# A hybrid mixer block: side work of the last block dealt anew, and the first rows of the output phase loaded ahead of w_out

## The chip, the cores and the metric

The kernel runs on one core of a Trainium2 chip. Its five engines work side by side, each through its own list of instructions in a fixed order: TensorE (PE, matmuls and transposes), VectorE (DVE), ScalarE (ACT), GpSimd (POOL) and the queue of SyncE (SP), which issues nearly all transfers between HBM and the core's memory. They wait for one another by semaphores. The metric is the device time of one execution in microseconds, the median of several runs.

## The reference

One decoder layer on x of 2048 tokens by 1024 channels, all in float32. A row norm with an adaptive scale and shift gives h; one projection `h @ w_in` gives the columns of three token mixers, which all read the same h:

```
A: gMLP.  y_a = gelu(u) * (tril(W_s) @ rms(gelu(v)) + b_s) * silu(z)      4 groups x 64, chunks of 128 tokens
B: mLSTM. q, k = silu(causal_conv(.)); per chunk of 128 tokens and 4 heads x 96:
          h = (intra-chunk weights @ v + w_inter * C q) / max(|den|, exp(-m));  C = decay * C + k^T v
          y_b = sigmoid(o) * rms(h) * silu(z)
C: stick-breaking attention, 6 heads x 64, strictly causal, with normed q and k:
          z = q k^T / 8;  a = sigmoid(z) * (product of sigmoid(-z) over the later keys)
          y_c = (a @ v) * silu(z_gate)
out = x + gate * (concat(y_a, y_b, y_c) @ w_out)
```

## The kernel before

The 2048 tokens are 16 tiles of 128, in three blocks of 5, 5 and 6 tiles (`BLOCKS`); the change touches the last block (tiles 10 to 15) and the phase behind it. Matmul operands are split in a high and a low part (the code has them side by side in `hT`, `wr`, `Kst`, `Vst`, `Qst`, `aT`, `wo`), so each product is three matmuls.

In a block, the attention goes through three **pairs** of heads (p = 0, 1, 2; the first, second and third pair below). `c_proj` projects q, k and v of the pair for the block's tiles; then `stick(p, ...)` does the attention in **units**: one tile of queries, one head, up to four tiles of keys, from the latest keys back. A unit is named pair_tile_head_firstkeytile, as in `z0_13_1_8`. With six tiles a pair has 44 units, the three pairs 132. A unit goes through `front` (TensorE: scores `z`; ScalarE: `bb` and `be`, two sigmoids; VectorE: a scan over `bb`, L414; then `be * bb`, L418, on VectorE and POOL by turns), `middle` (TensorE transposes into `at`; ScalarE and VectorE make the two parts of `aT`, L431 and L432), `back` (TensorE: `av`) and `fin` (`py`, `yc`, a store to `y_d`). The buffers `bb`, `be` and `aT` have four copies each.

Beside the attention runs **side work**: projections for the other two mixers, each one **chunk** of 6 tiles x 8 x 3 matmuls of 384 columns: `bqk_proj` (two chunks; PSUM tiles `pb`; its evacuation has four VectorE instructions per tile, L501 and L504, on `acc`), `bg_proj` (two, `pg`), `cz_proj` (`pcz`), `a_proj` (two, `pa`; a chain of VectorE, ScalarE and POOL instructions behind each tile, and two products `psp`/`gu` at its end) and `bv_proj` (`pv`). All these PSUM tiles and those of `c_proj` come from one pool of three buffers (`pproj`). Their weights come through `wr` (11 buffers, 8 used by a chunk). The list `fillers` says which chunks go beside which pair, and `interleave` takes steps from it in proportion to the cost so far; `behind` first finishes the pair's own `c_proj`. In the last block, `gating()` (the mLSTM gates' logarithms and maxima, small VectorE and ScalarE work on `g_all` and `g_row`) is mixed into the first pair and `first_chunk()` into the second.

The order of each engine's list is then fixed by a scheduler that places every instruction when its model finds it ready, by priority, so that later work can come earlier where an engine would be free: `bv_proj`, in the code behind the third pair, is placed within it.

The **output phase** (from `rs.close()` on) reuses the memory of the phase before: the pool `ld` lies where `stg`, `wr` and `hT` were, which side work uses to its end, and `wk`, `wo` and `wkb` where the attention's tiles were. `load(i)` fetches a tile's rows: `qk2`, `vb`, `gt`, `y`, `x` (`qk2` and `vb` only for i > 0); `wst` is `w_out` as loaded, which `split_wo` takes apart into `wo` (ScalarE casts the high part, VectorE and POOL subtract). Then, tile after tile, `mlstm(i)` runs the chunk of mixer B (`wT`, `s`, `pT`, `k`, `kw`, `i`, `nd`, `n`, `c`, `C`), `mixed(i)` makes the rows of y, `turned(i)` transposes them (`pty`, `yT`) and `out_proj(i)` multiplies with `wo` (`po`).

Of the kernel before, what the change touches and what calls it, by code (L numbers as in the profile page):

```python
# [33 lines left out]
def hybrid_block_kernel(ctx: ExitStack, tc: tile.TileContext, x, c, norm_g, w_ada, b_ada, w_in,  # L34
# [300 lines left out]
    def behind(cp, rest):  # L335

        yield from cp
        for m, c in enumerate(rest):
            if m == 6 and pend:
                evac_finish()  # L340
            yield c
        if pend:
            evac_finish()
# [128 lines left out]
    def stick_cost(t0, nb):  # L472
        return sum(2 * ((i + 1) * (2 * P / 2.4 + 218) + 215) for i in range(t0, t0 + nb))
# [34 lines left out]
    def bv_proj(t0, nb):  # L508
        with prio(HIGH[0]):
            wt = weights(w_in[0], [(OFF["bv"], 384)])  # L510
        for j in range(nb):
            i = t0 + j
            ps = pproj.tile([P, 512], F32, tag="proj", name=f"pv{i}")
            yield from proj_tc(ps[:, :384], wt, j, 384)
            vb = t512(f"vb{i}")
            vv = vb[:, 0:388].rearrange("p (h e) -> p h e", h=4)
            nc.gpsimd.memset(vv[:, :, 96:97], 1.0)
            nc.scalar.copy(vv[:, :, 0:96], ps[:, :384].rearrange("p (h e) -> p h e", h=4))
            nc.sync.dma_start(vb_d[i * P:(i + 1) * P, :], vb[:, 0:388])
# [230 lines left out]
    def run(g):  # L750
        for _ in g:
            pass
# [5 lines left out]
    def mix(a, n, g):  # L758
        for m, c in enumerate(a):
            yield c  # L760
            if m % n == n - 1:
                yield next(g, 0)
        yield from g

    def interleave(main, main_cost, side, side_cost):

        done = 0.0
        used = [0.0]
        side = iter(side)

        def step():
            c2 = next(side, None)
            if c2 is None:
                used[0] = 1e30
            else:
                used[0] += c2

        def until(j):
            with prio(-STK):
                while ready[0] < j:  # L780
                    step()

        need[0] = until
        while True:
            with prio(STK):
                c = next(main, None)
            if c is None:
                break
            done += c
            while used[0] < done / main_cost * side_cost:  # L790
                step()
        run(side)
# [46 lines left out]
    for b, nb in enumerate(BLOCKS):  # L839
        last = b == len(BLOCKS) - 1  # L840
        chunk = nb * KT * 3 * 384 / 2.4
        HIGH[0] = 0 if b == 0 else -4000
        fillers = [
            (chain(bqk_proj(t0, nb, 0), bqk_proj(t0, nb, 1), bg_proj(t0, nb, 0)), 3),
            (chain(bg_proj(t0, nb, 1), cz_proj(t0, nb), a_proj(t0, nb, 0)), 3),
            (a_proj(t0, nb, 1), 1),
        ]
        if b == 1:
            fillers[0] = (mix(fillers[0][0], 8, gate_gemv()), 3)
        if last:  # L850
            fillers[0] = (mix(fillers[0][0], 36, gating()), 3)
            fillers[1] = (mix(fillers[1][0], 14, first_chunk()), 3)
        for p in range(3):
            lead = min(nb, 2 + b)
            if p > 0:
                ready[0] = -1
                cp = c_proj(b, t0, nb, p)
                for _ in range(lead * KT + 1):
                    next(cp)
            cp_cost = 0 if b == 0 and p == 0 else (nb - lead) * KT * 3 * 384 / 2.4  # L860
            if b == 0 and p == 0:
                HIGH[0] = -400
            if p == 2 and not last:
                get_x(t0 + nb, 0)
                get_x(t0 + nb + 1, 1)
            interleave(stick(p, t0, nb), stick_cost(t0, nb), behind(cp, fillers[p][0]), cp_cost + fillers[p][1] * chunk)
        tail = bv_proj(t0, nb)
        if last:
            run(tail)
        else:  # L870
            t1, n1 = t0 + nb, BLOCKS[b + 1]
            ready[0] = -1
            cp = c_proj(b + 1, t1, n1, 0)
            lead = min(n1, 3 + b)
            for m, _ in enumerate(chain(tail, islice(cp, lead * KT + 1))):
                j = m // KT - 1
                if 0 <= j < n1 and m % KT in (1, 5):
                    if m % KT == 1 and j + 2 < n1:
                        get_x(t1 + j + 2, j + 2)
                    hT_half(t1 + j, j, m % KT // 4)  # L880
        t0 += nb
# [138 lines left out]
                next(side, None)  # L1020
        run(side)

    for kp in range(KT // 2):
        if kp == 1:
            load(0)
        nc.sync.dma_start(wst[kp], w_out[0, kp * 256:(kp + 1) * 256, :].rearrange("(a p) f -> p a f", p=P))
    load(1)
    C0 = wk.tile([96, 4, 97], F32, tag="C", name="C0")
    nc.sync.dma_start(C0.rearrange("p h e -> p (h e)"), c_d)
    CT = [C0]  # L1030
    wkb = ctx.enter_context(tc.tile_pool(name="wkb", bufs=2, side="right"))
    psO = ctx.enter_context(tc.tile_pool(name="psO", bufs=2, space=PSUM))
# [49 lines left out]
```

## Time and profile before

| | us |
|---|---|
| median of 3 runs (1473.59 to 1475.47) | 1473.66 |
| the profiled execution | 1471.23 |
| its span, first to last instruction | 1469.2 |
| TensorE busy (share) | 1393.4 (95%) |
| VectorE busy | 1018.8 (69%) |
| ScalarE busy | 676.5 (46%) |
| POOL busy | 647.6 (44%) |

In the span the last block's first pair lies at about 730 to 906 us, the second at 906 to 1078, the third at 1078 to 1209, and the output phase from there to the end. Times in rows are microseconds from the start of the span. Matmuls overlap in the array, so a matmul's own duration is longer than its distance to the next; distances between starts tell what it costs. The chain that ended last is 66% TensorE and 15% VectorE.

### The profile page before, as it was taken

What the parts mean: (1) busy time and instruction counts of PE and PEld (TensorE: products, weight loads), DVE (VectorE), ACT (ScalarE), POOL (GpSimd) and SP (SyncE); (2) the same over time, 40 slices, a digit from 0 to 9 for tenths busy, and PEclk for the clock granted to TensorE, in tenths of its full rate; (3) what the DMA queues carried; (4) which work ended last, traced back from release to release, by engine and by line L of the source; (5) the groups of instructions that cost most, each with busy time, mean ns of one, the idle gap of its engine ahead of it and who ended that gap; (6) DMA issues with size and microseconds to landing.
All of it is one profiled execution on the core that took longest, in us unless ns stands there. A gap on an engine that the chain in (4) does not pass through costs nothing.

```text
span 1469.2 us, 24957 instructions
## 1 busy us (share of the span) xinstructions
PE 1393.4 (95%) x8468; PEld 1298.2 (88%) x8468; DVE 1018.8 (69%) x1778; ACT 676.5 (46%) x1656; POOL 647.6 (44%) x1140
## 2 busy tenths in 40 slices
PE   5999999898999999999999999999999978999998
PEld 3789999798999999988999899989999867888887
DVE  6797554676995666588799976778778788444543
ACT  3364454453554444346467655556455655111110
POOL 4473553743433432554343343434445337435442
PEclk8999999999999999999999999999999999999999
DMA  9866776666535533633433344303432435555541
GB/s 324 293 204 206 237 228 197 208 202 236 191 128 176 198 116 124 222 100 127 148 105 126 104 146 137 102 15 120 157 102 69 156 113 153 178 160 154 175 154 58
DMA packets 187103, 233.19 MB, mean 159 GB/s; under 512 B 22714, under 2 KB 160344, under 8 KB 186976
## 3 DMA queue, kind: packets, MB, share of 16 engines
q1 hardware_dynamic: 186752, 231.59, 48.5%
q8 instruction: 67, 1.10, 0.3%
q14 instruction: 60, 0.49, 0.1%
q0 software_dynamic: 224, 0.02, 0.0%
HBM read 159.24 MB, written 72.31 MB: 158 GB/s over the span
## 4 chain that ended last, share of the span: by engine, by line
PE 66%; DVE 15%; DMA 6%; issue 5%; POOL 4%; ACT 2%; SPq 1%; POOLq 0%; DVEq 0%; ACTq 0%
DVE bb L414 5%; PE av L444 5%; PE at L429 4%; PE pc L297 4%; PE pc L299 4%; PE pc L298 4%; PE po L995 4%; PE po L997 3%; PE po L996 3%; PE pg L297 3%; PE pg L298 3%; PE pg L299 3%; DMA st<-in_w_in_dram 2%; PE z L401 2%; PE z L402 2%
## 5 line engine op out<-in xcount | busy, mean ns | idle before, releaser
L414 DVE TENSOR_TENSOR_SCAN bb<-bb,bb 128x513 f32<-128x513 f32 x144 | 191.3, 1328 | 25.5 <-ACT bb L406 24.7
L418 POOL TENSOR_TENSOR be<-be,bb 128x512 f32<-128x512 f32 (+3 forms) x120 | 133.0, 1108 | 132.9 <-DVE bb L414 81.4
L432 DVE TENSOR_TENSOR aT<-at,aT 128x512 fp32r<-128x512 f32 (+3 forms) x240 | 142.3, 598 | 39.8 <-ACT aT L431 39.1
L406 ACT ACTIVATE bb<-z 128x512 f32<-128x512 f32 (+3 forms) x240 | 130.2, 543 | 80.5 <-PE z L402 61.2
L444 PE MATMUL av<-aT,Vst 128*128 128x256 f32 x816 | 148.7, 295 | 17.8 <-DVE aT L432 13.0
L431 ACT CAST aT<-at 128x512 fp32r<-128x512 f32 (+3 forms) x240 | 126.6, 529 | 83.8 <-PE at L429 82.7
L444 PEld LDWEIGHTS av<-aT,Vst 128*128 128x128 f32 x816 | 119.9, 189 | 30.1 <-DVE aT L432 21.0
L429 PE MATMUL at<-ident,be 128*128 128x128 f32 x816 | 132.7, 274 | 5.2 <-DVE aT L432 2.3
L297 PE MATMUL pc<-wr,hT 128*128 128x384 f32 (+1 forms) x384 | 134.8, 355 | 2.8 <-ACT hT L290 1.3
L299 PE MATMUL pc<-wr,hT 128*128 128x384 f32 (+1 forms) x384 | 134.7, 351 | 1.6 <-DVE hT L291 1.5
L298 PE MATMUL pc<-wr,hT 128*128 128x384 f32 (+1 forms) x384 | 133.4, 347 | 0.0
L407 ACT ACTIVATE be<-z 128x512 f32<-128x512 f32 (+3 forms) x240 | 131.7, 549 | 0.0
L429 PEld LDWEIGHTS at<-ident,be 128*128 128x128 f32 x816 | 99.2, 141 | 14.2 <-DVE aT L432 3.7
L995 PE MATMUL po<-wo,yT 128*128 128x512 f32 x256 | 104.9, 410 | 0.3 <-ACT yT L984 0.3
L414 DVE TENSOR_TENSOR_SCAN bb<-bb 128x129 f32<-128x129 f32 (+3 forms) x96 | 87.1, 911 | 23.3 <-POOL bb L409 16.8
L405 POOL MEMSET bb<- 128x1 f32 x240 | 23.5, 100 | 177.6 <-DVE bb L414 123.6
L996 PE MATMUL po<-wo,yT 128*128 128x512 f32 x256 | 101.6, 397 | 0.0
L997 PE MATMUL po<-wo,yT 128*128 128x512 f32 x256 | 101.4, 399 | 0.0
L487 PE MATMUL pb<-hT,wr 128*128 128x320 f32 (+1 forms) x288 | 93.2, 324 | 1.2 <-DMA wr<-w_d 1.2
L489 PE MATMUL pb<-hT,wr 128*128 128x320 f32 (+1 forms) x288 | 92.1, 323 | 1.8 <-DVE wr L191 1.3
L297 PE MATMUL pa<-wr,hT 128*128 128x384 f32 x256 | 88.2, 347 | 5.1 <-DVE qk L360 2.4
L401 PE MATMUL z<-Kst,Qst 128*128 128x512 f32 (+3 forms) x240 | 90.2, 385 | 2.4 <-DVE Kst L371 1.6
(273 smaller groups left out, 3900.3 us busy)
## 6 DMA issues: line engine op xcount, KB each, us to landing
wr<-w_d SPq DMA_DIRECT2D x160, 384.0 KB, 5.6
w_d<-wr SPq DMA_DIRECT2D x80, 384.0 KB, 3.4
wad<-in_w_ada_dram SPq DMA_DIRECT2D x8, 1024.0 KB, 6.7
xo<-in_x_dram SPq DMA_DIRECT2D x16, 512.0 KB, 3.8
out_dram<-o SPq DMA_DIRECT2D x31, 256.0 KB, 2.9
xt<-in_x_dram SPq DMA_DIRECT2D x15, 512.0 KB, 4.9
st<-in_w_in_dram SPq DMA_DIRECT2D x60, 128.0 KB, 3.4
wr<-w_d SPq DMA_DIRECT2D x16, 392.0 KB, 6.2
```

The lines of the kernel that those rows point to most:

```text
L297: nc.tensor.matmul(ps, lhsT=hT[:, 0, k, cols], rhs=wt[k][:, 0, :W], start=k == 0, stop=False)
L298: nc.tensor.matmul(ps, lhsT=hT[:, 0, k, cols], rhs=wt[k][:, 1, :W], start=False, stop=False)
L299: nc.tensor.matmul(ps, lhsT=hT[:, 1, k, cols], rhs=wt[k][:, 0, :W], start=False, stop=k == KT - 1)
L407: nc.scalar.activation(be[:, :w], z[:, :w], AF.Sigmoid)
L414: nc.vector.tensor_tensor_scan(rev, rev, rev, carry.get((i, h), 1.0), ALU.mult, ALU.bypass)
L418: eng.tensor_tensor(be[:, :w], be[:, :w], bb[:, 1:w + 1], ALU.mult)
L429: nc.tensor.transpose(at[:, s, :], be[:, s * P:(s + 1) * P], ident)
L432: nc.vector.tensor_tensor(aT[:, :nb_, 1, :], at[:, :nb_, :], aT[:, :nb_, 0, :].bitcast(F32), ALU.subtract)
L444: nc.tensor.matmul(flat(av), lhsT=Vst[:, s0 + s, h, :], rhs=flat(aT[:, s]), start=(s0 + s == i), stop=(s0 + s == 0))
L995: nc.tensor.matmul(po, lhsT=yT[:, 0, k, :], rhs=wo[k][:, 0, cs], start=k == 0, stop=False)
L996: nc.tensor.matmul(po, lhsT=yT[:, 0, k, :], rhs=wo[k][:, 1, cs], start=False, stop=False)
L997: nc.tensor.matmul(po, lhsT=yT[:, 1, k, :], rhs=wo[k][:, 0, cs], start=False, stop=k == KT - 1)
```

## The change

Two edits. In the last block the side work is dealt anew: the first pair gets the two `bqk_proj` chunks (before: these and `bg_proj`'s first half), the second `bg_proj`'s two halves and `cz_proj` (before: `bg_proj`'s second half, `cz_proj` and `a_proj`'s first half), the third both `a_proj` and `bv_proj` (before: `a_proj`'s second half, with `bv_proj` in the code behind the pair). For the third pair `interleave` is told 0.8 of the attention's cost, so that the side work is to be used up at four fifths of it. The steps at which `gating()` is mixed in go from every 36th to every 24th. In the output phase the rows of tiles 0 and 1 are loaded first, and then `w_out`, in column halves: the four left halves and then the four right ones.

```diff
@@ -845,10 +845,16 @@
             (chain(bg_proj(t0, nb, 1), cz_proj(t0, nb), a_proj(t0, nb, 0)), 3),
             (a_proj(t0, nb, 1), 1),
         ]
+        if last:
+            fillers = [
+                (chain(bqk_proj(t0, nb, 0), bqk_proj(t0, nb, 1)), 2),
+                (chain(bg_proj(t0, nb, 0), bg_proj(t0, nb, 1), cz_proj(t0, nb)), 3),
+                (chain(a_proj(t0, nb, 0), a_proj(t0, nb, 1), bv_proj(t0, nb)), 3),
+            ]
         if b == 1:
             fillers[0] = (mix(fillers[0][0], 8, gate_gemv()), 3)
         if last:
-            fillers[0] = (mix(fillers[0][0], 36, gating()), 3)
+            fillers[0] = (mix(fillers[0][0], 24, gating()), 2)
             fillers[1] = (mix(fillers[1][0], 14, first_chunk()), 3)
@@ -863,11 +869,9 @@
-            interleave(stick(p, t0, nb), stick_cost(t0, nb), behind(cp, fillers[p][0]), cp_cost + fillers[p][1] * chunk)
-        tail = bv_proj(t0, nb)
-        if last:
-            run(tail)
-        else:
+            interleave(stick(p, t0, nb), stick_cost(t0, nb) * (0.8 if last and p == 2 else 1), behind(cp, fillers[p][0]), cp_cost + fillers[p][1] * chunk)
+        if not last:
+            tail = bv_proj(t0, nb)
@@ -1020,13 +1024,14 @@
-    for kp in range(KT // 2):
-        if kp == 1:
-            load(0)
-        nc.sync.dma_start(wst[kp], w_out[0, kp * 256:(kp + 1) * 256, :].rearrange("(a p) f -> p a f", p=P))
+    load(0)
     load(1)
     C0 = wk.tile([96, 4, 97], F32, tag="C", name="C0")
     nc.sync.dma_start(C0.rearrange("p h e -> p (h e)"), c_d)
+    for n in range(2):
+        for kp in range(KT // 2):
+            cs = slice(n * 512, (n + 1) * 512)
+            nc.sync.dma_start(wst[kp][:, :, cs], w_out[0, kp * 256:(kp + 1) * 256, cs].rearrange("(a p) f -> p a f", p=P))
```

The scheduler turns this into other lists. Three places follow; a row is the line, the operation, the tile it writes, those it reads, and the shape (x4: four in a row).

TensorE in the first pair, at the unit of tile 13, head 1, latest keys; `pb` is side work of `bqk_proj`, `z`, `at` and `av` belong to the attention. Before:

```order
L489 MATMUL pb4_10_1_10049<-hT_130,wr25_6_9744 128x384
L487 MATMUL pb4_10_1_10049<-hT_130,wr25_7_9746 128x384
L488 MATMUL pb4_10_1_10049<-hT_130,wr25_7_9746 128x384
L489 MATMUL pb4_10_1_10049<-hT_130,wr25_7_9746 128x384
L487 MATMUL pb5_10_0_10144<-hT_130,wr25_0_9732 128x384
L401 MATMUL z0_13_1_12_9912<-Kst_443,Qst_126 128x256
L402 MATMUL z0_13_1_12_9912<-Kst_443,Qst_126 128x256
L444 MATMUL av0_12_1_9752<-aT0_12_1_4_9776,Vst_444 128x256 x4
L429 MATMUL at0_13_0_12_9850<-ident_74,be0_13_0_12_9758 128x128 x2
L488 MATMUL pb5_10_0_10144<-hT_130,wr25_0_9732 128x384
L489 MATMUL pb5_10_0_10144<-hT_130,wr25_0_9732 128x384
L487 MATMUL pb5_10_0_10144<-hT_130,wr25_1_9734 128x384
```

And now, at the same unit:

```order
L401 MATMUL z0_13_1_12_9782<-Kst_443,Qst_126 128x256
L402 MATMUL z0_13_1_12_9782<-Kst_443,Qst_126 128x256
L401 MATMUL z0_13_1_8_9828<-Kst_443,Qst_126 128x512
L402 MATMUL z0_13_1_8_9828<-Kst_443,Qst_126 128x512
L444 MATMUL av0_12_1_9637<-aT0_12_1_4_9658,Vst_444 128x256 x4
L429 MATMUL at0_13_0_12_9729<-ident_74,be0_13_0_12_9643 128x128 x2
L401 MATMUL z0_13_1_4_9859<-Kst_443,Qst_126 128x512
L402 MATMUL z0_13_1_4_9859<-Kst_443,Qst_126 128x512
L444 MATMUL av0_12_1_9637<-aT0_12_1_0_9703,Vst_444 128x256 x4
L429 MATMUL at0_13_0_8_9759<-ident_74,be0_13_0_8_9675 128x128 x4
L460 MATMUL py0_12_9773<-fold_79,avt0_12_0_9608 128x64
L444 MATMUL av0_13_0_9770<-aT0_13_0_12_9732,Vst_444 128x256 x2
```

The side matmuls between the units are gone from this stretch: from `z0_13_0_8` to `z0_14_0_0`, 11 units, no projection stands in TensorE's order.

TensorE in the third pair, where the side work ends; `pv15` is the last tile of `bv_proj`. Before:

```order
L298 MATMUL pv15_14742<-wr33_7_14595,hT_130 128x384
L299 MATMUL pv15_14742<-wr33_7_14595,hT_130 128x384
L444 MATMUL av2_13_0_13857<-aT2_13_0_12_13822,Vst_444 128x256 x2
L460 MATMUL py2_12_13860<-fold_79,avt2_12_1_13834 128x64
L401 MATMUL z2_13_1_0_13970<-Kst_443,Qst_126 128x512
L402 MATMUL z2_13_1_0_13970<-Kst_443,Qst_126 128x512
L429 MATMUL at2_13_0_4_13900<-ident_74,be2_13_0_4_13813 128x128 x4
L444 MATMUL av2_13_0_13857<-aT2_13_0_8_13854,Vst_444 128x256 x4
```

And now:

```order
L298 MATMUL pv15_14504<-wr33_7_14150,hT_130 128x384
L299 MATMUL pv15_14504<-wr33_7_14150,hT_130 128x384
L429 MATMUL at2_14_0_0_14403<-ident_74,be2_14_0_0_14302 128x128 x4
L401 MATMUL z2_15_0_12_14508<-Kst_443,Qst_126 128x512
L402 MATMUL z2_15_0_12_14508<-Kst_443,Qst_126 128x512
L444 MATMUL av2_14_0_14325<-aT2_14_0_4_14366,Vst_444 128x256 x4
L429 MATMUL at2_14_1_12_14445<-ident_74,be2_14_1_12_14348 128x128 x3
L401 MATMUL z2_15_0_8_14549<-Kst_443,Qst_126 128x512
```

The end of the side work moved from ahead of the unit `z2_13_1_0`, with 17 of 44 units to come, to ahead of `z2_15_0_12`, with 8 to come.

ScalarE where the output phase begins; `yc2_15` is the attention's last tile, `wT` the weights of mixer B, `yT` the transposed rows of tile 0. Before:

```order
L462 COPY yc2_15_14578<-py2_15_14575 128x128
L663 ACT_TABLE_LOAD
L663 ACTIVATE wT1_14927<-wT1_14927,gT_96 128x128 x4
L663 ACTIVATE wT2_15044<-wT2_15044,gT_96 128x128 x4
L984 CAST yT0_14849<-pty0_0_14850 128x512
L984 CAST yT0_14849<-pty0_1_14857 128x512
L901 CAST wo0_14799<-wst0_14807 128x512
```

And now:

```order
L462 COPY yc2_15_14768<-py2_15_14765 128x128
L663 ACT_TABLE_LOAD
L663 ACTIVATE wT1_14931<-wT1_14931,gT_96 128x128 x3
L988 CAST yT0_14853<-pty0_0_14854 128x512
L988 CAST yT0_14853<-pty0_1_14861 128x512
L905 CAST wo0_14799<-wst0_14807 128x512
L905 CAST wo1_14800<-wst0_14807 128x512
```

`yT` moved ahead of the second tile's exponentials and of one of the first tile's; those follow behind all sixteen casts of `wo`. On TensorE, in the same way, `n1`, `s2`, `k3` and `i3` of mixer B moved from ahead of the first `po` to behind it.

## Rows read from the trace of the kernel before

**Rows 1.** Windows: length; busy us (count) of PE, PEld, DVE, ACT, POOL; clock; DMA; GB/s.

```profile
730.00:906.00 176.00, 172.39 (x1089) 165.52 (x1088) 144.43 (x243) 110.72 (x239) 70.71 (x143) 1.00 0.35 113
906.00:1078.00 172.00, 168.67 (x1070) 161.39 (x1069) 128.07 (x213) 88.49 (x212) 69.32 (x136) 1.00 0.33 106
1078.00:1209.00 131.00, 118.93 (x755) 108.61 (x754) 108.87 (x170) 80.39 (x187) 54.60 (x113) 1.00 0.33 111
1160.00:1209.00 49.00, 37.21 (x240) 29.47 (x239) 44.05 (x57) 31.85 (x67) 18.68 (x35) 1.00 0.51 178
971.00:981.00 10.00, 7.61 (x50) 5.68 (x50) 10.00 (x17) 7.58 (x19) 4.70 (x13) 1.00 0.01 2
1209.00:1219.00 10.00, 7.49 (x64) 6.85 (x63) 5.07 (x11) 5.52 (x14) 4.72 (x6) 0.98 0.93 253
1219.00:1226.00 7.00, 7.00 (x31) 6.32 (x31) 7.00 (x8) 7.00 (x14) 6.41 (x6) 0.54 0.45 138
```

**Rows 2.** Timeline of TensorE in the third pair: start, duration, instruction.

```profile
1150.67 0.39 PE L401 MATMUL z<-Kst,Qst 128*128 128x512 f32 x1
1150.90 0.40 PE L402 MATMUL z<-Kst,Qst 128*128 128x512 f32 x1
...
1160.49 0.34 PE L298 MATMUL pv<-wr,hT 128*128 128x384 f32 x1
1160.67 0.34 PE L299 MATMUL pv<-wr,hT 128*128 128x384 f32 x1
...
1205.82 0.60 PE L429 MATMUL at<-ident,be 128*128 128x128 f32 x4
1206.17 0.72 PE L444 MATMUL av<-aT,Vst 128*128 128x256 f32 x4
```

**Rows 3.** VectorE's groups by form in 740 to 1209: count, busy, mean, idle before.

```profile
L414 DVE TENSOR_TENSOR_SCAN bb<-bb,bb 128x513 f32<-128x513 f32 x94 | 125.1, 1331 | 16.3 <-ACT bb L406 15.7
L432 DVE TENSOR_TENSOR aT<-at,aT 128x512 fp32r<-128x512 f32 x108 | 72.5, 677 | 17.5 <-ACT aT L431 17.4
L418 DVE TENSOR_TENSOR be<-be,bb 128x512 f32<-128x512 f32 x44 | 31.2, 710 | 0.6
L501 DVE SCALAR_TENSOR_TENSOR acc<-xb,prm,acc 128x384 f32<-128x384 f32 x36 | 23.8, 662 | 1.1 <-ACT acc L497 0.9
```

**Rows 4.** Waits in 1160 to 1210: total us, times, longest.

```profile
POOL y L968 <- DMA y<-yb_d: 1.5, 1, 1.5
```

**Rows 5.** Timeline of TensorE: last av group, first output matmul, the second tile's first.

```profile
1207.82 0.74 PE L444 MATMUL av<-aT,Vst 128*128 128x256 f32 x4 [0.28 <-DVE aT L432]
...
1222.02 0.77 PE L995 MATMUL po<-wo,yT 128*128 128x512 f32 x1
...
1246.32 0.47 PE L995 MATMUL po<-wo,yT 128*128 128x512 f32 x1
```

**Rows 6.** Timeline of ScalarE at the seam.

```profile
1213.73 1.28 ACT L663 ACT_TABLE_LOAD   x1 [3.10 <-DMA wT<-m_d]
1215.02 2.45 ACT L663 ACTIVATE wT<-wT,gT 128x128 f32<-128x128 f32 x8
1217.38 1.04 ACT L984 CAST yT<-pty 128x512 fp32r<-128x512 f32 x2
```

**Rows 7.** Timeline of POOL: its last three subtractions for the left halves.

```profile
1221.82 4.21 POOL L902 TENSOR_TENSOR wo<-wst,wo 128x512 fp32r<-128x512 f32 x3
```

**Rows 8.** Timeline of SyncE's queue: first and last load, and C0.

```profile
1161.04 0.38 SPq L1026 DMA_DIRECT2D wst<-in_w_out_dram  x1
...
1180.30 0.32 SPq L921 DMA_DIRECT2D gt<-gate_d  x1
...
1208.79 0.48 SPq L1029 DMA_DIRECT2D C<-c_d  x1
```

**Rows 9.** The page's DMA issues: count, KB each, us to landing.

```profile
wad<-in_w_ada_dram SPq DMA_DIRECT2D x8, 1024.0 KB, 6.7
xo<-in_x_dram SPq DMA_DIRECT2D x16, 512.0 KB, 3.8
```

## The prediction

> **What bounds the kernel now.** I read the page's busy shares first (TensorE 95% busy, so only holes in TensorE are worth anything), then windows over the last block's three attention pairs and the start of the output phase, then the timelines of the engines at its seams. In the first and second pair TensorE stands idle for 3.6 us and 3.3 us, in the third for 12.1 us [rows 1]. Nearly all of that is one stretch: the last side matmul (`pv15`) starts at 1160.67 [rows 2], and from then the attention runs alone. In 1160 to 1209 VectorE is busy for 44.1 of 49 us and TensorE for 37.2 [rows 1]: 11.8 us of holes, with VectorE in charge. A full unit costs VectorE one scan (1.33 us), one `aT` subtraction (0.68) and half of the `be` products (0.71 / 2): 2.37 us [rows 3]. TensorE needs less for it: two 512-column matmuls 0.23 us apart and eight small ones at 0.09 to 0.14 each [rows 2], which I take as 0.12: about 1.44 us. So a unit with nothing beside it costs TensorE 0.9 us of waiting.
>
> But VectorE is nearly full early too. In 730 to 906 it is busy for 144 of 176 us [rows 1], and there `bqk_proj` alone adds 36 taps of 0.66 us, 24 us [rows 3], while `bg_proj` has a single product a tile there.
>
> The second place is the seam to the output phase: the last attention matmul group starts at 1207.82 and the first output matmul at 1222.02 [rows 5]. ScalarE waits there 3.1 us for `wT`, spends 2.45 us on eight exponentials, and only then casts `yT` at 1217.38 [rows 6].
>
> **The change, part by part.** *The deal of the side work.* A chunk is 144 matmuls of 384 columns, 0.17 to 0.18 us apart [rows 2]: 24.4 us of TensorE. `bg_proj`'s first half leaves the first pair, one `a_proj` leaves the second for the third, and `bv_proj` stays in the third. In the order before, 17 units still follow `pv15`; in the changed order 8 do, so the 4/5 is what the order does (36 of 44 units).
>
> What this is worth I worked out pair by pair. I cut the 132 units of the block into groups of four, added for each group TensorE's issue times (384 columns 0.17, 512 columns 0.226, small ones 0.124) and VectorE's mean durations per form over the instructions that the order puts between the two scans, and took the larger. Before, the three pairs have TensorE sums of 167, 162 and 106 us, VectorE sums of 158, 139 and 113, and larger-of-two sums of 178, 170 and 124: 472 together. The trace took 470 between the same scans, so the method holds for before. Changed, TensorE has 147, 149 and 139, VectorE 157, 122 and 131, and the larger-of-two sums are 172, 156 and 147: 475.
>
> So the first pair gives up 20 us of TensorE work but gets only 6 us shorter, since VectorE keeps all its work. The order shows where: from z0_13_0_8 on, 11 units run with no side matmul between them, since `acc`'s evacuation stands late in VectorE's order, after `gating`, and the three PSUM buffers of the projections are then full. Over twelve units there, 801 to 831 us in the trace of before, the sums are now 18.7 us for TensorE and 35.1 for VectorE. The hole has moved from the end of the third pair to the middle of the first. The net is +3.3 us. With groups of 2 to 11 units, and with TensorE's costs 6% lower, the same sum gives -3.3 to +6.6: these are my bounds.
>
> *Rows ahead of w_out.* POOL waited 1.5 us for `y` of tile 0 before its product [rows 4], while `be` products stood behind it on its queue; that `y` was issued after the first 1 MB of `w_out`. In the changed order these rows come first and the product stands one unit after the loads start. I take -1.0 us (bounds -1.5 and 0; the lower is the row, nothing is gained if VectorE has slack there).
>
> *w_out in halves.* Eight transfers of 512 KB take the place of four of 1 MB. The nearest rows are 3.8 us for 512 KB and 6.7 us for 1 MB [rows 9]: one after the other 30.4 against 26.8 us, 3.6 us more. What hides it: before, the loads' first and last issue are 19 us apart (1161.04 and 1180.30 [rows 8]). Now 8 units follow `pv15`, 8 x 2.37 = 19 us, and the drain, from the last scores to the last `av` group, is some 8 us more: 27 us, and a further 10 us pass before the first cast of `wo`. I take 0. If the cover is gone, up to 3.6 us show. The Trainium skill ("DMA: Bandwidth & Descriptors", section Bandwidth) says to batch transfers to 1 MiB or more, as smaller ones pay a larger share of fixed cost, and so speaks against the halves; by it these loads get longer, which is the case of late loads below. The trace agrees in direction (138 GB/s against 157, from the same two rows).
>
> *The start of the output phase.* Three things move in the order. `gu1`'s two products and stores leave the seam; I count that at nothing, since `avt` behind them waits for ScalarE anyway. On ScalarE `yT` comes after 3 exponentials in place of 8: 5 x 0.3 = 1.5 us earlier. On TensorE `n1`, `s2`, `k3` and `i3` no longer stand ahead of the first output matmul, so it waits for `yT` and the first `wo` halves alone: I get 9.5 us after the last `av` group, against 14.2 [rows 5]. From there POOL's `wo` subtractions set the pace, whose first halves end at 1226.03 [rows 7], 18.2 us after that group; they come 1.5 to 2 us earlier. The second tile's output starts at 1246.32 [rows 5], 38.5 us after the last `av` group; what lies in between shows 2.5 us of idle TensorE in 1209 to 1219 and 7 us at a mean granted clock of 0.54 in 1219 to 1226 [rows 1]. Counting the changed order through to `po1` I get 33 to 35 us. I take -3.5 us. Bounds: 0, if `wT1` (whose load still waits for the end of attention and now queues behind more rows) holds `yT` where it was; -8, if all idle time and half-clock time goes.
>
> **The sum.** +3.3 - 1.0 - 3.5 = -1.2 us. The profiled execution took 1471.23 us for a span of 1469.2, so it would take 1470.0; the median of the runs is 1473.66, 2.4 us above the profiled one, and becomes 1472.5. Changes under 0.2% (2.9 us) can't be told from none here.
>
> **Rivals.** *Faster: the first pair's backlog is worked off under the change-over.* After each pair comes `c_proj` of the next, with TensorE full and VectorE less so. If VectorE's late `acc` work slides in there, groups of 8 or 11 units are the right ones (-3.3 to -1.2) and the sum is -3.3 - 1.0 - 3.5 = -7.8: 1466. For it: TensorE is full in 730 to 906 except for 3.6 us though VectorE has 144 us of work. Against: TensorE is in order, and 11 units without side work stand in its order in one run.
>
> *Slower: every stretch pays for itself.* The attention has four `bb` and four `be` buffers, so the engines can't drift apart by more than about three units, 7 us of VectorE work. The empty run holds 35.1 - 18.7 = 16 us of excess, beyond that. Then +6.6 is right, and the seam gives half of its estimate: +6.6 - 1.0 - 1.8 = +3.8: 1477.5; without the seam's gain 1479. It decides if TensorE's idle time in the first pair rises by more than 15 us. Against: groups of four reproduce before within 2 us.
>
> *The clock falls in the empty run.* In 971 to 981, 7.6 of 10 us busy, the granted clock stayed at 1.00; after 1209 to 1219, 7.5 of 10 us busy, it was 0.54, part of the time the lower level of 1.2 GHz [rows 1]. At half clock 18.7 us of TensorE work becomes 37, against 35.1 of VectorE: 2 us at worst. It widens the range only.
>
> *Late w_out (slower).* If the halves land after the first casts of `wo`, the 3.6 us show: 1476.
>
> *No effect as said* is excluded by the order: the side work does end after 36 units.
>
> **How the numbers follow.** Forecast, within 0.2%: 0.40. Faster: 0.34. Slower: 0.23 for stretches that pay for themselves and 0.03 for late loads, 0.26. The single terms' bounds add to 1473.66 - 3.3 - 1.5 - 8 = 1461 and 1473.66 + 6.6 + 0 + 3.6 = 1484; both ends need everything to go one way, so for 8 in 10 I take 1464 to 1480.5. The likeliest case's own range is 1470.7 to 1476.6.
>
> **What would show it.** Right: TensorE's idle time in the first pair rises to 10 to 20 us, in one run of 11 units with VectorE at 95% or more; the third pair's end has 5 to 6 us of holes in place of 11.8; first output matmul 9 to 11 us after the last `av` group; no wait of POOL for `y`. Wrong: the first pair shorter by 12 us or more (faster), or the third longer by over 27 us (slower); `wo` casts waiting for a DMA; first output matmul still 14 us after.

## The result, and the profile after

The changed kernel takes 1487.77 us (median of 4 runs, 1486.61 to 1489.93) beside 1474.27 for the kernel before on the same chip (4 runs): 1.0095 times as long, 95% interval 1.0082 to 1.0108, or 13.5 us more. The forecast was 1472.5 (1464 to 1480.5). The profiled execution spans 1484.9 us against 1469.2, so 15.7 us are to be found there.

I cut both executions at the last matmul of the last `av` group: 1208.3 us before, 1216.8 after. The attention part is 8.5 us late, and the output phase behind it takes 268.1 us instead of 260.9, another 7.2. The first was forecast at about +2 to +3, the second at -3.5.

Windows of the changed kernel over the three pairs, and three short ones; the columns are those of [rows 1].

```profile
731.00:899.00 168.00, 157.77 (x967) 145.93 (x967) 143.05 (x239) 106.94 (x234) 68.99 (x132) 0.98 0.32 102
899.00:1057.00 158.00, 155.52 (x999) 149.36 (x998) 114.40 (x172) 84.23 (x188) 65.30 (x125) 1.00 0.32 107
1057.00:1187.00 130.00, 129.72 (x806) 125.39 (x805) 99.74 (x184) 71.42 (x178) 52.73 (x118) 1.00 0.26 81
1187.00:1217.00 30.00, 22.90 (x145) 19.16 (x144) 24.79 (x31) 17.75 (x37) 10.79 (x17) 0.94 0.86 285
801.00:811.00 10.00, 4.67 (x23) 3.40 (x23) 8.67 (x15) 9.04 (x15) 3.23 (x8) 0.85 0.01 2
811.00:821.00 10.00, 9.21 (x52) 7.49 (x51) 9.38 (x17) 7.12 (x17) 4.07 (x8) 0.81 0.03 8
1225.00:1235.00 10.00, 6.25 (x26) 4.74 (x25) 10.00 (x6) 9.07 (x20) 9.60 (x8) 0.83 0.16 47
```

TensorE is idle for 10.2 us in the first pair, 2.5 in the second, 7.4 in the third: 20.1, where [rows 1] had 19.0. So the holes moved, as forecast, and were not filled. The first pair's hole lies in 801 to 811 (4.67 of 10 us busy), and around it the granted clock falls to 0.85 and 0.81, so part of 801 to 821 ran at the lower level of 1.2 GHz. The third pair is full up to 1187. In 1225 to 1235, in the output phase, VectorE is busy all the time with 6 instructions, POOL for 9.6 us with 8.

TensorE's timeline in the changed kernel; it answers to [rows 5].

```profile
1197.48 1.16 PE L667 MATMUL s<-qk 96*128 96x128 f32 x8 [1.44 <-DMA qk<-qkT_d]
...
1216.31 0.74 PE L444 MATMUL av<-aT,Vst 128*128 128x256 f32 x4 [0.76 <-DVE aT L432]
...
1224.85 0.49 PE L999 MATMUL po<-wo,yT 128*128 128x512 f32 x1
1227.27 0.50 PE L1000 MATMUL po<-wo,yT 128*128 128x512 f32 x1 [1.92 <-DVE wo L906]
...
1237.58 0.50 PE L1000 MATMUL po<-wo,yT 128*128 128x512 f32 x1 [4.41 <-DVE wo L906]
```

The first output matmul comes 8.5 us after the last `av` group (14.2 before), a little better than I said. But then tile 0's output stops twice for a `wo` subtraction of VectorE. The chain of waits shows which one:

```profile
1228.83 8.70 DVE wo L906
1237.58 0.50 PE po L1000
```

The timelines of POOL and of VectorE; POOL's lines answer to [rows 4, 7].

```profile
1194.14 1.01 POOL L972 TENSOR_TENSOR y<-y,gt 128x384 f32<-128x384 f32 x1 [2.99 <-issue]
...
1225.40 2.96 POOL L906 TENSOR_TENSOR wo<-wst,wo 128x512 fp32r<-128x512 f32 x2 [0.57 <-ACT wo L905]
1228.32 1.28 POOL L965 TENSOR_TENSOR C<-C,decay 96x388 f32<-96x388 f32 x1
1229.56 7.41 POOL L906 TENSOR_TENSOR wo<-wst,wo 128x512 fp32r<-128x512 f32 x6
```

```profile
1225.51 1.70 DVE L906 TENSOR_TENSOR wo<-wst,wo 128x512 fp32r<-128x512 f32 x1
...
1227.61 10.52 DVE L906 TENSOR_TENSOR wo<-wst,wo 128x512 fp32r<-128x512 f32 x3
1238.05 0.55 DVE L673 TENSOR_TENSOR kw<-k,ex 128x384 f32<-128x384 f32 x1
1238.51 2.48 DVE L906 TENSOR_TENSOR wo<-wst,wo 128x512 fp32r<-128x512 f32 x4
1240.92 0.68 DVE L668 TENSOR_TENSOR pT<-s,wT 128x512 f32<-128x512 f32 x1
```

One subtraction (`wo4`, the second of the three) started at 1228.83, while POOL's decay product `C` ran, and took 8.7 us; alone it takes 0.68 (the four at 1238.51 are 0.6 apart). It ended at 1237.5, with POOL's row of six subtractions (1229.56 to 1236.97, 1.24 us apart, no gap). ScalarE had cast all its input by then. The second thing to see is the last line: tile 1's first product, `pT1`, starts at 1240.92, 24 us after the last `av` group. Before it stood ahead of the `wo` subtractions, 8 us after that group.

### The profile page after: what moved, and what is told of

Its sections match the earlier page's. It is cut to its first block, busy times and chain, and to the rows that moved or that the text cites. A ratio compares the mean times of both kernels' runs of the same rounds, so it can differ in the third digit from the quotient of the medians.

```text
span 1484.9 us, 24969 instructions
## 1 busy us (share of the span) xinstructions
PE 1401.5 (94%) x8468; PEld 1302.1 (88%) x8468; DVE 1023.1 (69%) x1778; ACT 678.9 (46%) x1656; POOL 649.6 (44%) x1140
## 4 chain that ended last, share of the span: by engine, by line
PE 69%; DVE 12%; DMA 6%; issue 5%; POOL 3%; ACT 3%; SPq 1%; DVEq 0%; POOLq 0%; ACTq 0%
PE av L444 5%; PE at L429 4%; PE po L999 4%; PE po L1000 4%; PE po L1001 4%; PE pc L297 3%; PE pc L299 3%; PE pc L298 3%; DVE bb L414 3%; PE pg L297 3%; PE pg L298 3%; PE pg L299 3%; PE z L401 2%; PE z L402 2%; DMA st<-in_w_in_dram 2%
```

## Experiments

Theories: **A**, POOL's uninterrupted row of subtractions keeps VectorE's from running. **B**, the seam's loss comes with the new loads. **C**, tile 1's chain now stands behind the `wo` subtractions. **D**, the changed first pair is held up by where `gating` stands; **E**, by VectorE's work as a whole; **F**, by serial steps. In the table the pairs run from the first VectorE scan of one pair to that of the next (the third to the last scan); "drain" is from there to the last `av` matmul, "rest" from there to the end, all from one profiled execution of each kernel. The time is the median of the runs, the ratio is to the kernel before on the same chip, with its 95% interval (for the two single runs there is none).

| kernel | pair 1 | pair 2 | pair 3 | drain | rest | time | ratio |
|---|---|---|---|---|---|---|---|
| before | 175.8 | 172.3 | 122.2 | 8.2 | 260.9 | 1474.3 | 1 |
| changed | 168.1 | 157.8 | 149.6 | 10.3 | 268.1 | 1487.8 | 1.0095 (1.0082 to 1.0108) |
| deal_only | 168.3 | 157.7 | 148.2 | 9.6 | 271.6 | 1488.2 | 1.0095 (1.0081 to 1.0109) |
| loads_only | 174.7 | 172.3 | 123.4 | 9.2 | 260.9 | 1476.2 | 1.0012 (0.9999 to 1.0024) |
| wo_all_vector | 168.2 | 158.5 | 151.4 | 9.4 | 264.9 | 1485.9 | 1.0079 (1.0064 to 1.0094) |
| wo_right_vector | 168.6 | 157.7 | 150.0 | 9.4 | 264.4 | 1482.1 | 1.0049 (1.0035 to 1.0064) |
| chain_first | 168.2 | 158.8 | 149.7 | 9.6 | 263.8 | 1486.4 | 1.0080 (1.0065 to 1.0095) |
| chain_first_wo_vector | 169.1 | 157.7 | 149.5 | 10.3 | 258.3 | 1478.8 | 1.0032 (1.0020 to 1.0044) |
| spread_only | 175.0 | 172.2 | 125.6 | 9.2 | 266.0 | 1481.1 | 1.0047 (1.0033 to 1.0062) |
| before_wo_vector | 175.2 | 172.4 | 122.3 | 9.0 | 258.9 | 1471.1 | 0.9987 (0.9972 to 1.0002) |
| before_wo_left_vector | 174.6 | 172.4 | 123.2 | 9.0 | 264.8 | 1480.0 | 1.0048 (1.0034 to 1.0062) |
| gating_36 | 170.3 | 155.7 | 149.8 | 10.3 | 263.6 | 1483.3 | 1.0065 (1.0052 to 1.0078) |
| gating_10 | 172.7 | 162.2 | 150.0 | 10.3 | 260.8 | 1490.8 | 1.0116 (1.0100 to 1.0132) |
| deal_332 | 175.3 | 149.1 | 144.9 | 10.3 | 259.2 | 1472.2 | 0.9987 (0.9977 to 0.9998) |
| taps_changed | 164.5 | 157.7 | 149.8 | 9.6 | 259.2 | 1473.7 | |
| taps_before | 174.1 | 172.5 | 123.7 | 8.2 | 261.5 | 1473.1 | |
| deal_332_old_loads | 174.5 | 150.8 | 141.6 | 9.6 | 256.2 | 1467.7 | 0.9962 (0.9947 to 0.9977) |

**deal_only** (the changed kernel, its last hunk undone)

```
-    load(0)
+    for kp in range(KT // 2):
+        if kp == 1:
+            load(0)
+        nc.sync.dma_start(wst[kp], w_out[0, kp * 256:(kp + 1) * 256, :]...
     load(1)
...
-    for n in range(2):
...
```

> The kernel before with the deal of the side work alone; its loads stay as they were (1 MB pieces of w_out, tile 0 behind the first piece). In its program POOL's order at the seam already has the six wo subtractions in one row that the changed kernel has. Theory A (POOL's uninterrupted row of two-input subtractions keeps VectorE's wo subtraction from running, 8.7 us for one in the changed kernel): the last av group comes 6 to 9 us later than before, one of VectorE's wo subtractions takes 5 us or more, the seam loses 5 to 8 us, and the time is 1486 to 1490. Theory B (the seam's loss comes with the loads: rows first, halves of w_out, gate_bc and m_d late): no wo subtraction above 2 us, the seam as before, only the attention's 6 to 9 us: 1480 to 1484.

Measured: A. The deal alone loses everything: the rest takes 271.6 us, one `wo` subtraction 8.67. B falls: the loads don't make the seam's loss.

**loads_only** (the kernel before with that hunk alone)

> The kernel before with the new loads alone; the deal stays. POOL's order at the seam keeps its two affine_selects between the wo subtractions, as before. Theory A: VectorE's wo subtractions stay at 0.7 to 1.8 us, the time is 1471 to 1475 (-3 to +1). Theory B: the seam loses its 7 us here too, about 1481.

Measured: the rest is unchanged, 260.9. The time is 1.5 us up, at the edge of what can be told, not 1 us down. What got worse is a wait that the kernel before doesn't have: tile 1's scores stand in TensorE's order amid the attention, and they wait for their `qk2` load. The load and the scores before, then in loads_only:

```profile
1167.95 0.47 SPq L914 DMA_DIRECT2D qk<-qkT_d  x1
...
1185.10 0.83 PE L667 MATMUL s<-qk 96*128 96x128 f32 x6
```

```profile
1164.32 0.43 SPq L914 DMA_DIRECT2D qk<-qkT_d  x1
...
1171.04 1.16 PE L667 MATMUL s<-qk 96*128 96x128 f32 x8 [2.03 <-DMA qk<-qkT_d]
```

The load is issued 3.6 us sooner, but the scores stand 14 us sooner, 6.7 us behind it in place of 17.

**wo_all_vector** and **wo_right_vector** (the changed kernel)

```
-        (nc.gpsimd if k % 2 else nc.vector).tensor_tensor(wo[k][:, 1, cs], ...
+        nc.vector.tensor_tensor(wo[k][:, 1, cs], ...
```

In wo_right_vector the choice is `nc.gpsimd if k % 2 and n == 0 else nc.vector`: POOL keeps four left halves.

> The changed kernel with all 16 wo subtractions on VectorE, none on POOL. Theory A: each takes 0.7 us or a little more, the fourth left half ends within 8 us of the first output matmul instead of 13, the seam's 7 us come back: 1479 to 1482, the attention's 8.5 us stay. Theory B: no change or up to 5 us slower (eight more subtractions of 0.62 us on VectorE): 1487 to 1493.

> The changed kernel with POOL doing four wo subtractions (left halves 1, 3, 5, 7) and VectorE twelve: POOL's longest row is then two, not six. Theory A: the longest VectorE wo subtraction shrinks from 8.7 us to about 2 x 1.24 + 0.7 = 3.2 us, and the time lies at 1480 to 1483. Theory B: 1487 to 1491.

Groups of VectorE's `wo` subtractions: shortest, median and longest in ns, first and last start. wo_all_vector, then wo_right_vector:

```profile
L906 DVE TENSOR_TENSOR wo<-wst,wo x16: 675/678/847, 1228.0 to 1238.2; 128x512 fp32r<-128x512 f32 x16
```

```profile
L906 DVE TENSOR_TENSOR wo<-wst,wo x12: 674/680/3809, 1228.6 to 1240.9; 128x512 fp32r<-128x512 f32 x12
```

Measured: the longest subtraction goes from 8.7 us (POOL's row of six) to 3.8 (two) and 0.85 (none). A is shown, but the time came back only in part: the rest falls to 264.9 and 264.4, not to 261. `pT1` still started 19.8 and 21.8 us after the last `av` group. As times, wo_right_vector (1482.1, inside my range) is clearly better than the changed kernel; wo_all_vector (1485.9, above my 1479 to 1482) is not, as the two intervals overlap. That led to C.

**chain_first** (the changed kernel) and **chain_first_wo_vector** (with wo_all_vector's edit too)

```
     run(turned(0))
+    ahead = chunk_ahead(1)
+    for _ in range(4):
+        next(ahead)
     for k in range(KT):
         split_wo(k, 0)
...
-    ahead = chunk_ahead(1)
-    for _ in range(6):
+    for _ in range(2):
```

> The changed kernel with the first four steps of tile 1's mLSTM chain (weights, scores and pT1, kw1, i1, n1) written ahead of the wo split and of tile 0's first output; POOL keeps its eight wo subtractions. From the last av group to the end the kernel before took 260.9 us, the changed one 268.1; pT1's product started 8.1 us after that group before, 24.1 us in the changed kernel. Theory C (behind the lockout a second cause: tile 1's chain now stands behind the wo subtractions on VectorE): pT1 starts within 10 us of the last av group, that last stretch shrinks to 261 to 264 us although one VectorE wo subtraction still takes over 3 us, and the time is 1480 to 1484. Theory A alone (the lockout is all of it): the stretch stays at 266 or more, 1486 to 1490.

> The same chain ahead, and all wo subtractions on VectorE: both causes taken away. If A and C together are the seam's loss, the stretch after the last av group comes to 258 to 262 us and the time to 1477 to 1481, that is the time before plus the attention's 5 to 9 us. If something else of the new order holds the seam (late loads, the clock), the stretch stays above 264 and the time above 1483.

VectorE's timeline in chain_first:

```profile
1229.31 0.68 DVE L668 TENSOR_TENSOR pT<-s,wT 128x512 f32<-128x512 f32 x1
1229.91 0.55 DVE L966 TENSOR_TENSOR C<-c,C 96x388 f32<-96x388 f32 x1
1230.38 11.87 DVE L906 TENSOR_TENSOR wo<-wst,wo 128x512 fp32r<-128x512 f32 x3
```

Measured: `pT1` is back at 8.9 us after the last `av` group and the rest at 263.8, though one subtraction still takes 9.3 us. Either cause alone gives 3 to 4 us of the rest, both together 9.8: with both taken away it is 258.3, less than before, and 1478.8 us, 9 less than the changed kernel. What is left over the kernel before, 5 us, is the attention with its drain, 8 us longer, less the 2.6 us that the rest gained. The median of chain_first (1486.4) lies above my 1480 to 1484, and its interval overlaps the changed kernel's: its attention part was 12 us late in the profiled execution, 4.3 of them ahead of the block, in code that was not changed. One value of the rest is not exact to 3 us: the five kernels with both of these edits have 258.3 to 263.6, though their output phase is written alike. So the parts of the two causes are rough; that the two together make up the loss is clear in the times.

**spread_only** (the kernel before, in its last block)

```
+        if last:
+            fillers[2] = (chain(a_proj(t0, nb, 1), bv_proj(t0, nb)), 2)
...
-            interleave(stick(p, t0, nb), stick_cost(t0, nb), ...
+            interleave(stick(p, t0, nb), stick_cost(t0, nb) * (0.8 if last and p == 2 else 1), ...
...
```

> The kernel before with no chunk moved between the pairs: bv_proj is put behind the last a_proj in the third pair's interleave and both are spread over four fifths of it; first and second pair and the loads as before. By the larger-of-two sums its attention is 1 us shorter than before (470.8 against 471.7), so if the moved chunks cost the attention's 5 to 9 us, the last av group is at 1205 to 1210 here. In its order pT1 stays ahead of the wo subtractions, but POOL has six of them in a row behind wT3: theory A expects one VectorE wo subtraction of 4 us or more, and 261 to 265 us after the last av group; C alone 260 to 262. Time 1472 to 1478. If late side work by itself (not the moved chunks) lengthens the attention, the last av group is past 1213 and the time past 1479.

Measured: a miss, 1481.1. The attention is 2 to 3 us longer, not 1 shorter, and the rest takes 266.0 though `pT1` stands early and no `wo` subtraction is long. Timelines of VectorE and POOL:

```profile
1225.06 0.90 DVE L902 TENSOR_TENSOR wo<-wst,wo 128x512 fp32r<-128x512 f32 x1
1225.88 9.97 DVE L676 SCALAR_TENSOR_TENSOR sm<-nd,ex 128x4 f32<-128x4 f32 x1
1235.77 1.28 DVE L902 TENSOR_TENSOR wo<-wst,wo 128x512 fp32r<-128x512 f32 x2
```

```profile
1227.86 0.63 POOL L660 TENSOR_SCALAR_AFFINE_SELECT wT<-wT 128x512 f32<-128x512 f32 x1
1228.46 7.37 POOL L902 TENSOR_TENSOR wo<-wst,wo 128x512 fp32r<-128x512 f32 x6
```

What was shut out this time was an instruction on 4 elements, 0.15 us elsewhere: it took 9.97 us and ended with POOL's row, in spite of the affine_select ahead of POOL's last six. So size is no protection, and everything in VectorE's order waits behind the victim.

**before_wo_vector** (the kernel before with wo_all_vector's edit) and **before_wo_left_vector** (the left halves on VectorE, the right ones shared, tile 1's chain with a priority 400 ahead)

```
-        (nc.gpsimd if k % 2 else nc.vector).tensor_tensor(wo[k][:, 1, cs], ...
+        (nc.gpsimd if k % 2 and n == 1 else nc.vector).tensor_tensor(wo[k][:, 1, cs], ...
...
-    for _ in range(6):
-        next(ahead)
+    with prio(-400):
+        for _ in range(6):
+            next(ahead)
```

> The kernel before with all 16 wo subtractions on VectorE. Its own VectorE wo subtractions took up to 1.76 us beside POOL's; theory A expects 0.7 us each here and the four left halves of VectorE plus POOL's done sooner: 1470 to 1475. If VectorE's eight more subtractions (8 x 0.6 us) hold up tile 1's chain (hh1 now stands behind them), 1474 to 1479.

> The kernel before with its left wo halves all on VectorE, the right ones shared as before (POOL has four subtractions left, not in one row with others), and tile 1's chain given a better place in the order. Theory A and C: no VectorE instruction at the seam above 3 us, the stretch after the last av group 256 to 259 us against 260.9, time 1469 to 1473. If four subtractions of POOL in a row still shut VectorE out for 4 us or more, 261 us and 1473 to 1476.

Measured: the first as expected, 1471.1; the interval just reaches no change. The second, at 1480.0, is a miss. POOL has four subtractions left and an affine_select between the first two, and one subtraction of VectorE took 6.41 us; the rest is 264.8. Also the other way round: beside VectorE's subtractions, POOL's decay product `C` took 3.69 us instead of 0.83.

**gating_36** and **gating_10** (on chain_first_wo_vector; 10 in place of 36)

```
-            fillers[0] = (mix(fillers[0][0], 24, gating()), 2)
+            fillers[0] = (mix(fillers[0][0], 36, gating()), 2)
```

> The chain_first_wo_vector kernel (both causes of the seam's loss taken away, 1478.8) with one number put back: gating is dealt a step after every 36 side matmul groups of the first pair, as before, not after every 24; the deal of 2, 3, 3 stays. Theory D (the first pair gets only 7 us shorter for 20 us less TensorE work because gating and the late acc work stand in one stretch on VectorE): the larger-of-two sums by groups of four give 165.7 us for the first pair against 172.3, so about 6 us come back: first pair 162 to 164 us measured instead of 169, time 1471 to 1475. Theory E (the first pair is bound by VectorE's total or by ScalarE, wherever gating stands): first pair 167 to 170, time 1477 to 1481.

> The same kernel with gating dealt a step after every 10 side matmul groups, so early in the first pair. Theory D: by the same sums 159.5 us for the first pair and 159.7 for the second, 8.6 us less than with 24 together: 1468 to 1474. Theory E: 1477 to 1481.

Measured: D falls. The first pair takes 170.3 and 172.7 us, not less than 169. With 36 the hole only moves later; windows of gating_36:

```profile
801.00:811.00 10.00, 10.00 (x65) 9.79 (x64) 8.46 (x13) 6.18 (x14) 3.63 (x10) 1.00 0.21 61
...
821.00:841.00 20.00, 15.68 (x80) 11.98 (x80) 18.89 (x26) 14.44 (x31) 7.50 (x15) 0.83 0.02 4
841.00:861.00 20.00, 16.24 (x98) 14.00 (x99) 19.52 (x34) 12.10 (x24) 7.69 (x17) 1.00 0.31 95
```

The time of gating_36 says nothing on D: its attention is no longer than that of chain_first_wo_vector (475.8 us against 476.3), and the 4.5 us that it takes more lie in the rest (263.6 against 258.3). In gating_10 the attention itself is 8.6 us longer.

**taps_changed** (on chain_first_wo_vector) and **taps_before** (on the kernel before); both leave out two of the three taps of `bqk_proj`'s convolution in the last block

```
-                for tap in range(3):
+                for tap in range(1 if t0 == 10 else 3):
```

> The chain_first_wo_vector kernel with two of the three convolution taps of bqk left out in the last block (24 VectorE instructions of 0.66 us, 16 us; q and k of the last block's mLSTM come out wrong). Theory E (VectorE bounds the changed first pair as a whole): the first pair, 169 us there, comes to 153 to 160 us, TensorE's idle time in it falls from 10 us to under 5. Theory F (serial steps of gating and of the evacuations bound it, not VectorE's work): 165 to 169 us.

> The kernel before with the same two taps left out in the last block. TensorE fills its first pair (3.6 us idle in 176), so 16 us less VectorE work should give 3 us at most there: 172.5 to 175 us by both theories. If it gives 8 us or more, VectorE bounded the first pair before too, and the sums are wrong in another way.

Measured: 16 us less VectorE work shorten the changed first pair by 4.6 us and that of before by 1.7 (one run each). E is not enough. TensorE is still idle for 9.6 us in 731 to 898 (8.7 in chain_first_wo_vector), most of it in score matmuls that wait for ScalarE's `be`; line of taps_changed in that window:

```profile
L401 PE MATMUL z<-Kst,Qst 128*128 128x512 f32 (+3 forms) x44 | 18.8, 431 | 6.2 <-ACT be L407 6.2
```

That is near F's 165 to 169, but which serial step sets it I did not isolate.

**deal_332** (on chain_first_wo_vector) and **deal_332_old_loads** (with the loads of before)

```
-                (chain(bqk_proj(t0, nb, 0), bqk_proj(t0, nb, 1)), 2),
-                (chain(bg_proj(t0, nb, 0), bg_proj(t0, nb, 1), cz_proj(t0, nb)), 3),
+                (chain(bqk_proj(t0, nb, 0), bqk_proj(t0, nb, 1), bg_proj(t0, nb, 0)), 3),
+                (chain(bg_proj(t0, nb, 1), cz_proj(t0, nb)), 2),
                 (chain(a_proj(t0, nb, 0), a_proj(t0, nb, 1), bv_proj(t0, nb)), 3),
...
-            fillers[0] = (mix(fillers[0][0], 24, gating()), 2)
-            fillers[1] = (mix(fillers[1][0], 14, first_chunk()), 3)
+            fillers[0] = (mix(fillers[0][0], 36, gating()), 3)
+            fillers[1] = (mix(fillers[1][0], 14, first_chunk()), 2)
```

> The same seam (tile 1's chain ahead, wo subtractions on VectorE), but only one chunk moved: the first pair keeps bqk and the first half of bg and gating after 36 groups, as before; the second has the other half of bg and cz; the third both a_proj and bv_proj over four fifths. By the sums of four 177.9, 148.9 and 143.3 us, 470 together against 475 of the changed deal and 472 of before. Theory D: first pair 175 to 177 measured, third 146 to 148, last av group 4 to 6 us earlier than with the changed deal, time 1472 to 1476. If the third pair pays more than its TensorE sum again (149 to 150 measured for 147.3 in the changed deal), 1475 to 1479.

> The deal_332 kernel with the loads as they were before (1 MB pieces, tile 0 behind the first). If the loads are worth nothing, as loads_only said (0 to 2.4 per mille slower), 1470 to 1474; if the rows ahead of w_out are what the early part of the seam needs with late side work, 1475 to 1479.

Measured: as the sums said, 469.3 us of attention against 474 to 478 with the changed deal. With the old loads it takes 1467.7 us, 0.9962 of the kernel before (0.9947 to 0.9977): this version beats both, and lies below the 1470 to 1474 that I expected. The new loads cost about 4 us here (4.4 by the medians, on two chips; 3.7 by the ratios), with 3.3 us in the third pair and 3.0 in the rest of the profiled executions, again with the wait for `qk2`; TensorE in deal_332, then in deal_332_old_loads:

```profile
1192.37 2.00 PE L667 MATMUL s<-qk 96*128 96x128 f32 x8 [2.48 <-DMA qk<-qkT_d]
```

```profile
1204.38 1.06 PE L667 MATMUL s<-qk 96*128 96x128 f32 x8
```

## Why the prediction was wrong

**The deal, +3.3: right mechanism, too small.** Scan to scan the changed attention takes 475.5 us against 470.3: +5.2, and +3.9 to +7.8 in the five other kernels that keep this deal with its 24 (one of them above my bound of +6.6). The rest of the 8.5 us are 1.1 ahead of the block, in code that was not changed, and 2.1 in the drain. By pairs I had said -6, -14 and +23; it was -7.7, -14.5 and +27.4. The third is the one that was off. TensorE sets its pace for 130 of its 160 us (129.72 busy), and there my count of TensorE's time was short. In its 149.6 us TensorE waited 4.1 (lines of the changed kernel, then of before, scan to scan):

```profile
L444 PE MATMUL av<-aT,Vst 128*128 128x256 f32 x138 | 23.9, 291 | 1.7 <-DVE avt L450 1.2 <-DVE aT L432 0.4
...
L401 PE MATMUL z<-Kst,Qst 128*128 128x512 f32 (+3 forms) x43 | 17.6, 409 | 1.0 <-ACT be L407 1.0
...
L667 PE MATMUL s<-qk 96*128 96x128 f32 x8 | 1.2, 288 | 1.4 <-DMA qk<-qkT_d 1.4
```

```profile
L444 PE MATMUL av<-aT,Vst 128*128 128x256 f32 x138 | 24.8, 298 | 8.5 <-DVE aT L432 7.2 <-DVE avt L450 1.3
...
L401 PE MATMUL z<-Kst,Qst 128*128 128x512 f32 (+3 forms) x42 | 17.7, 422 | 0.5 <-ACT be L407 0.4
```

So it worked for 145.5 us, where the sum had 139; before it worked for 122.2 - 9.0 = 113.2, where the sum had 106. One term of it is the matmul of 384 columns: from start to start, less the waits, the 481 of them in the changed pair took 86.5 us, 0.18 each, where the sum took 0.17; that is 4.7 us of the 6.5. The same 7 us were missing before, hidden since VectorE's 113 was the larger. That the method met 470 before was thus no proof of its parts, and I had tried TensorE's costs lower, not higher. The sums are also no guide to a moved serial step: for the first pair they gave -7 and -13 us in gating_36 and gating_10, and it got 1 and 4 us longer.

**The first pair** went as I wrote: 20 us of work less, 7 to 8 us shorter, a hole of 10.2 us (forecast 10 to 20). VectorE was busy for 87 and 94% in it, not 95. The clock did fall there, which I had priced at 2 us at worst. The slower rival was nearest in size and in its mark "third longer by over 27"; its other mark, 15 us more idle time in the first pair, failed (6.6), and at 1477.5 to 1479 it was still 9 us short.

**Rows ahead of w_out, -1.0: wrong sign.** POOL's wait for tile 0's `y` did not go: the rows are issued later too (from 1187.89, against 1161.04 for the first load in [rows 8]), and POOL waited 2.99 us for them (the line at 1194.14 above, put down to "issue"; in chain_first the same wait, 3.01 us, is put down to a load of `y`). With the deal alone it is 0.26 us, against 1.5 in [rows 4]: the new loads brought it back. And I had counted only POOL's wait: TensorE's in-order wait for `qk2` (1.2 to 2.7 us in all ten kernels with the new loads, none in the seven with the old) stood in none of my terms. loads_only measures the whole at +1.5, with an interval that just reaches no change.

**w_out in halves, 0: held.** No cast of `wo` waited for a load.

**The start of the output phase, -3.5: the step that failed, by 10.7 us.** The early part was right: `yT` was cast at 1223.24, 1223.24 - 1216.31 = 6.9 us after the last `av` group (9.6 in [rows 6]), and the first output matmul came at 8.5. Two sentences failed. "POOL's `wo` subtractions set the pace" took 1.4 us for each from [rows 7] and nothing for VectorE's; in POOL's new order nothing stands between six of them, with the product `C` directly ahead, and VectorE's was shut out for 8.7 us. And "`n1`, `s2`, `k3` and `i3` no longer stand ahead of the first output matmul" I booked as a gain, without following what they had been there for: tile 1's chain, from `pT1` to `yT1`, went behind the `wo` work. I counted 33 to 35 us to tile 1's first output matmul; it came at 1260.54, 44.2 us after the last `av` group (38.5 before).

The kernel before also has POOL's and VectorE's subtractions side by side, and they take turns there; on VectorE from its timeline, then on POOL:

```profile
1227.62 0.16 DVE L678 RECIPROCAL sm<-sm 128x4 f32<-128x4 f32 x1
1227.71 0.53 DVE L953 TENSOR_TENSOR nd<-n,nd 128x388 f32<-128x388 f32 x1
1228.15 1.24 DVE L902 TENSOR_TENSOR wo<-wst,wo 128x512 fp32r<-128x512 f32 x1
...
1230.88 1.25 DVE L676 SCALAR_TENSOR_TENSOR sm<-nd,ex 128x4 f32<-128x4 f32 x1
```

```profile
1218.09 0.83 POOL L961 TENSOR_TENSOR C<-C,decay 96x388 f32<-96x388 f32 x1 [0.68 <-DVE C L962]
1219.53 1.27 POOL L902 TENSOR_TENSOR wo<-wst,wo 128x512 fp32r<-128x512 f32 x1 [0.61 <-ACT wo L901]
...
1227.05 6.83 POOL L902 TENSOR_TENSOR wo<-wst,wo 128x512 fp32r<-128x512 f32 x4
```

The reciprocal (one input) and the `nd` sum (one input from PSUM, the memory that matmuls write to) run at full speed beside POOL; the two with both inputs in SBUF, the core's main memory, take 1.24 us, and POOL's four 1.71 each. That was in the trace of before, and I read past it.

What goes with one or the other shows when all 17 traces are read from 1195 us on. In each of the six kernels with a long victim (3.8 to 9.97 us), the victim was issued while POOL's product `C` ran, with another POOL product directly behind it. That happened 14 times in all, and 14 times VectorE waited past that next product too, and past the rest of the row where there was one. In the 48 other cases where a VectorE instruction was held up by over 0.25 us with a second POOL instruction directly behind the first (`wo`, `y` or `o`), it ran as soon as the first ended; so in the changed kernel itself, where `wo0` at 1225.51 took 1.70 us beside POOL's two. In the kernel before, `C` ended at 1218.92, 0.6 us ahead of the first `wo` on POOL. So the row sets how long the victim waits, and `C` at its head goes with the waiting. That is read from the traces; no run moved `C` alone, and why it differs is open.

The Trainium skill ("SBUF — State Buffer", section Who interferes with whom) says that a VectorE instruction with two SBUF inputs contends with a GpSimd instruction that reads SBUF, that one with at most one SBUF input, outside the two-port modes, does not, that the pair of ports which the two engines share is an exclusive lock, and that issue order decides who blocks. The rows agree on who is hit. By that rule, as I read it, a victim would wait for the one POOL instruction that was issued first, an estimate of 1.3 us at most from the rows above; the 48 cases agree with it, but the victims beside `C` waited for rows of two to seven subtractions (3.81 to 9.97 us).

## What to carry to other kernels

Where VectorE and POOL work side by side on the same memory, look at how many of the one's instructions stand in a row in the new order, and at what stands at the head of the row, not at their mean duration: the other may wait for the whole row. When instructions no longer stand ahead of a critical one, ask whose chain they were, and where that ends now. And a model that meets a total has still to be tried on its parts: here TensorE's 7 missing microseconds lay under VectorE's until the work was moved.

## What was not expected of the hardware

- An instruction of VectorE on 128x4 elements took 9.97 us beside seven POOL subtractions in 1226.6 to 1235.8, through an affine_select of POOL that lay between two of them.
- Beside the same work the engines sometimes take turns (before, loads_only: 1.8 us at most) and sometimes one is shut out until the other's row ends (six of the kernels here). With another POOL product directly behind, every instruction issued beside POOL's product `C` was shut out (14 of 14), and none of the 48 issued beside another; what is special about `C` is open.
- It goes both ways, again with `C`: alone it takes 0.83 us, beside VectorE's subtractions 3.0 to 4.4 us, in eight kernels that have twelve or all sixteen of them on VectorE. No other POOL instruction at the seam took over 2 us.
